# Four operand sums of w made in two halves each, and the row sums of |w| held back: a change to a matmul, tanh and multiply kernel

## The chip, the cores and the metric

The kernel runs on one core of a Trainium2 chip. The metric is the device time of one execution in microseconds (us), lower is better. The unchanged kernel has a median of 300.54 us over 6 runs (300.2 to 300.82).

## What is computed

```python
batch, m, k, n = 16, 512, 1024, 768
# x: (16, 512, 1024), w1 and w2: (1024, 768), all float32
y1 = np.matmul(x, w1)
y2 = np.matmul(x, w2)
return (np.tanh(y1) * y2).astype(np.float32)
```

With batch and m flattened, x has 8192 rows, which are 64 tiles of 128 rows. The inner dimension 1024 is 8 slices of 128.

## The kernel before

**Operands.** x and w are brought to f16. `wh` holds both weights, w1 in columns 0 to 767 and w2 in columns 768 to 1535, slice by slice. Slice k of w1 is loaded by the step `La{k}` and cast by `ca{k}`; `Lb{k}` and `cb{k}` do the same for w2 (L332 to L347). The loads are issued in the order x0 a0 x1 a1 x2 a2 x3 a3 a4 to a7 b0 to b7 (L538), so all of w1 comes ahead of w2. A cast may run on DVE or on ACT.

**Head.** The first six row tiles are multiplied plainly: `m{mt}{t}F{k}` is a matmul of 512 columns, `m{mt}{t}G{k}` one of the other 256, t = 0 for w1 and 1 for w2 (L447 to L449). x tiles 0 to 3 arrive as f32, are turned by TensorE (`PT{mt}{h}`, half h, L351) and moved from PSUM to SBUF as f16 by `e{mt}{h}` (a copy, L342 on ACT, L344 on DVE; `e10` is the first half of x tile 1). Tiles 4 and 5 are turned by `PT4`, `PT5` (L361). Then tanh of the first product (`thF`, `thG`, L455) and the multiplication with the second (`muF`, `muG`, L459) follow.

**Triples.** Row tiles 6 to 62 go in 19 groups of three (triples). Each triple is computed by a bilinear scheme with 15 products instead of the 18 that the plain way needs (`C_OPS`). A product is 4 matmuls of 128x512 (L477). Its operands are blocks of x and of w, or signed sums of blocks. Sums of x blocks (`S`, L434) are made anew for each triple. The eleven sums of w blocks (`B`, L424, listed in `B_SUMS`) are made once, 128x2048 f16 each, on DVE. Between the products, ACT makes copies of PSUM banks (`copy`, `seed`, L483) and tanh (L495), and DVE makes additions (L492) and the last multiplication (L500). The last row tile is plain again.

A w block is half of the slices by 512 columns. Blocks 1 and 8 are columns 0 to 511 of w1, 2 and 16 the same of w2, and 4 and 32 take the last 256 columns of w1 beside the last 256 of w2. So the first 256 columns of the sums 5, 36, 37 and 45 depend on w1 alone. In their other 256 columns, a block 4 or 32 takes part, and with it w2.

**Range check.** For every x tile and every slice of w, ACT sums absolute values (`D{mt}` and `awa{k}`, `awb{k}`, L390), an activation with an accumulator that writes a scratch tile `junk`. All these sums are looked at once, at the end; a general path would follow if they were out of range.

**Order.** A planner (`Planner.run`) lays out all steps before anything is issued. Each step has engines with a cost, a due time, steps that it needs, and steps that it only has to stand behind (`behind`). The planner fills each engine's queue in order of due times; the order of TensorE's products is fixed by hand (`PE_ORDER`). Each engine then runs its queue strictly in order. The eight PSUM banks are handed out by the planner: a bank is reused when its last reader is planned to be through. DMA loads of x (POOL queue), DMA transposes and stores (SP queue) have their own places in the plan.

Of the kernel before, what the change touches and what calls it, by code (L numbers as in the profile page):

```python
# [77 lines left out]
class Planner:  # L78
# [13 lines left out]
    def op(self, name, engines, due, needs, fn, *args, behind=(), issued=(), chains=(), xfer=0.0, latency=None, seeds=False):  # L92


        assert name not in self.ops, name
        self.ops[name] = dict(engines=engines, due=due, needs=[n for n in needs if n], behind=[n for n in behind if n], issued=[n for n in issued if n], fn=fn, args=args,
                              chains=chains, xfer=xfer, latency=latency, seeds=seeds)
        for c in chains:
            self.chains.setdefault(c, {"left": 0, "bank": None, "end": 0.0, "by": ""})["left"] += 1
# [134 lines left out]
def kernel(  # L234
# [19 lines left out]
    B, M, K = x.shape  # L254
    _, N = w1.shape
    KO = K // P
    KH = KO // 2
# [6 lines left out]
    LOW, HIGH = 512.0, 1024.0  # L264
    XT_BUFS, S_BUFS, O_BUFS, C_BUFS, WF_BUFS = 4, 2, 3, 2, 12
    WARM = 21
    AFTER = (0, 0, 0)
    SOON = {"S": 3.0, "D": 3.0}
    GATE = 2
# [31 lines left out]
    wsum = {v: once.tile([P, KH, F], f16, name=f"b{v}") for v, *_ in B_SUMS}  # L301
# [6 lines left out]
    pin = tc.keep_in_program_order  # L308
    engine = {"dve": nc.vector, "act": nc.scalar, "pool": nc.gpsimd, "sp": nc.sync}
    plan = Planner(8)  # L310
    op = plan.op
# [87 lines left out]
    def split(a):  # L399
        return a.rearrange("p k (t g) -> p k t g", t=2)  # L400

    def w_block(v):

        if v in wsum:
            return split(wsum[v])
        bit = v.bit_length() - 1
        rows = wh[:, bit // 3 * KH:(bit // 3 + 1) * KH, :]
        if bit % 3 == 2:
            return rows.rearrange("p k (t n) -> p k t n", t=2)[:, :, :, F:]
        return split(rows[:, :, bit % 3 * N:bit % 3 * N + F])  # L410
# [9 lines left out]

    OP = {"add": ALU.add, "sub": ALU.subtract}

    def w_sum(e, v, a, b, how):
        pin(engine[e].tensor_tensor(w_block(v), w_block(a), w_block(b), OP[how]))  # L424

    def x_operand(i, v):
        if v & (v - 1):
# [113 lines left out]
    for n, what in enumerate(loads):  # L541
# [5 lines left out]
        else:  # L547
            t = "ab".index(what[0])
# [3 lines left out]
    for a, t, k in slices:  # L552
        op(f"c{a}{k}", {"dve": 0.5, "act": 0.74}, 6 + 1.3 * k + 9.5 * t,
           [f"L{a}{k}"], cast_w, t, k)
        op(f"aw{a}{k}", {"act": 0.92}, 80 + 10 * (t * KO + k), [f"c{a}{k}"], abs_w, t, k)
    for mt in range(4):
        for h in range(2):
            due = 5 + 2.3 * mt + 0.1 * h
# [27 lines left out]
    def reuse_out(mt):  # L586
        return [f"st{mt - 3 * O_BUFS}"] if HEAD + 3 * O_BUFS <= mt else []
# [20 lines left out]
    for mt in list(range(4, HEAD)) + list(range(MT - TAIL, MT)):  # L608
# [6 lines left out]
        for n, (t, which) in enumerate(parts):  # L615
            last = plain(mt, t, which, (which, mt, t), lambda k: base + 1.7 * n + 0.2 * k,
                         behind=[plan.strict[FILL[n]]] if tail else ())
# [23 lines left out]
    for v, a, b, how in B_SUMS:  # L641
        needs = []
        for u in (a, b):
            if u in wsum:
                needs.append(f"B{u}")
            else:
                bit = u.bit_length() - 1
                needs += [f"c{s}{k}" for s in ("a", "b", "ab")[bit % 3] for k in range(bit // 3 * KH, (bit // 3 + 1) * KH)]
        op(f"B{v}", {"dve": 1.13}, None, needs, w_sum, v, a, b, how)

    def x_needs(i, v):
        if v & (v - 1):
# [12 lines left out]
    for i in range(TRIPLES):  # L665
        for v, a, b, how in A_SUMS:
            op(f"S{v}.{i}", {"pool": 1.12} if v in ON_POOL and i >= POOL_FROM else {"dve": 0.34}, None, x_needs(i, a) + x_needs(i, b), x_sum, i, v, a, b, how,
               behind=[f"{r}.{i - S_BUFS}" for r in a_readers[v]] if i >= S_BUFS else [])
# [3 lines left out]
        for o in C_OPS:  # L672
            name, kind, needs = o[:3]
            needs = [f"{n}.{i}" for n in needs]
# [22 lines left out]
            if kind in ("t", "th"):  # L697
                lo, n = (0, F) if kind == "t" else (F, G)
                op(f"{name}.{i}", {"act": 0.5 if n == F else 0.29}, due, needs, c_tanh, i, r, o[4], lo, n, o[5],
                   behind=reuse_out(mt), chains=chains)  # L700
# [11 lines left out]
    for mt in range(MT - TAIL - 3):  # L712
        op(f"st{mt}", {"sp": 0.05}, 52 + 4.33 * mt if mt >= HEAD else 250 + 5 * mt, outs[mt], store, mt,
           issued=[f"T{MT - 1}"] if mt < HEAD else [f"p{AFTER[(mt - HEAD) % 3]}.{(mt - HEAD) // 3 + 1}"], xfer=1.1)
    for mt in range(4, MT):
# [8 lines left out]
        else:  # L724
            op(f"T{mt}", {"sp": 1.35}, None, [f"L{mt}"], transpose, mt,
               issued=[f"T{mt - 1}"] if mt > BY_PE else [],
               behind=xt_readers[mt - 3 * XT_BUFS] if mt >= 3 * XT_BUFS else [], xfer=1.45, latency=2.2)
# [11 lines left out]
    pin(nc.vector.memset(ones, 2.0 ** -12))  # L739
    for n in range(WARM):  # L740
        pin(nc.tensor.matmul(banks[n % 8][:, n // 8 % 2 * 2 * P:][:, :2 * P], ones.bitcast(bf16)[:, :P], ones.bitcast(bf16), start=True, stop=True))  # L741
# [106 lines left out]
```

## Time and profile before

| what | value |
|---|---|
| median of 6 runs | 300.54 us |
| time of the profiled execution | 300.36 us |
| its span, first to last instruction | 298.5 us |
| mean granted TensorE clock | 0.997 |
| TensorE matmul (PE) busy | 292.6 us, 98% |
| TensorE weight load (PEld) busy | 139.8 us, 47% |
| VectorE (DVE) busy | 240.4 us, 81% |
| ScalarE (ACT) busy | 219.7 us, 74% |
| GpSimd (POOL) busy | 32.7 us, 11% |
| sums of w, L424 | 11 of 128x2048, 1215 to 1227 ns each, 24.5 to 51.8 us into the span |
| sums of abs(w), L390 | 16, median 844 ns each and a readout of 194 ns, 7.6 to 78.8 us into the span |

PE is TensorE's matmul row and PEld its weight loads, SPq, ACTq and POOLq are queues that issue DMAs. Times in the views are counted from the start of the span. A line such as L477 is the place in the kernel that issued an instruction.

### The profile page before, as it was taken

What the parts mean: (1) busy time and instruction counts of PE and PEld (TensorE: products, weight loads), DVE (VectorE), ACT (ScalarE), POOL (GpSimd) and SP (SyncE); (2) the same over time, 40 slices, a digit from 0 to 9 for tenths busy, and PEclk for the clock granted to TensorE, in tenths of its full rate; (3) what the DMA queues carried; (4) which work ended last, traced back from release to release, by engine and by line L of the source; (5) the groups of instructions that cost most, each with busy time, mean ns of one, the idle gap of its engine ahead of it and who ended that gap; (6) DMA issues with size and microseconds to landing.
All of it is one profiled execution on the core that took longest, in us unless ns stands there. A gap on an engine that the chain in (4) does not pass through costs nothing.

```text
span 298.5 us, 4459 instructions
## 1 busy us (share of the span) xinstructions
PE 292.6 (98%) x1418; PEld 139.8 (47%) x1418; DVE 240.4 (81%) x497; ACT 219.7 (74%) x438; POOL 32.7 (11%) x67
## 2 busy tenths in 40 slices
PE   8999999999999999999999999999999999999994
PEld 6656544444444444444444444444444444444442
DVE  1308999988988887888978979797898989888854
ACT  2879989999886868767787767777766777773641
POOL 0021211211002011110101111011011101000000
PEclk9999999999999999999999999999999999999998
DMA  7999999999999999999999999999999999996053
GB/s 282 409 399 210 161 175 147 185 136 263 190 191 124 294 238 236 247 299 128 246 86 210 250 246 248 202 236 140 195 232 252 124 284 233 167 374 267 19 231 124
DMA packets 82584, 64.79 MB, mean 217 GB/s; under 512 B 63616, under 2 KB 64128, under 8 KB 82560
## 3 DMA queue, kind: packets, MB, share of 16 engines
q1 hardware_dynamic: 73344, 47.20, 67.3%
q0 software_dynamic: 8640, 15.73, 37.9%
q10 hardware_dynamic: 576, 1.57, 1.3%
q8 instruction: 11, 0.18, 0.3%
q14 instruction: 13, 0.11, 0.2%
HBM read 39.85 MB, written 25.17 MB: 218 GB/s over the span
## 4 chain that ended last, share of the span: by engine, by line
PE 97%; ACT 1%; DVE 0%; issue 0%
PE bank L477 82%; PE bank L449 12%; PE bank L741 2%; ACT xT L342 1%; PE bank L351 1%; PE bank L361 0%; ACT junk L390 0%; DVE o L459 0%; DVE ones L739 0%; PE bank L515 0%
## 5 line engine op out<-in xcount | busy, mean ns | idle before, releaser
L477 PE MATMUL bank<-b,s 128*128 128x512 f16 x608 | 140.8, 379 | 0.0
L477 PEld LDWEIGHTS <-s 128*128 128x128 f16 x760 | 74.3, 98 | 89.6
L492 DVE TENSOR_TENSOR bank<-bank,s 128x512 f32<-128x512 f32 x95 | 66.2, 697 | 29.1 <-ACT s L483 22.2
L483 ACT ACTIVATE s<-bank 128x512 f32<-128x512 f32 x95 | 55.3, 597 | 42.2 <-PE bank L477 39.3
L390 ACT ACTIVATE junk<-xh 128x1024 f16<-128x1024 f16 x60 | 63.3, 1055 | 0.2
L500 DVE TENSOR_TENSOR o<-o,bank 128x256 f32<-128x256 f32 (+1 forms) x114 | 60.7, 548 | 2.2 <-ACT o L495 1.7
L477 PEld LDWEIGHTS <-xT 128*128 128x128 f16 x380 | 37.2, 98 | 44.6 <-issue 0.2
L477 PE MATMUL bank<-b,xT 128*128 128x512 f16 x228 | 55.4, 379 | 0.0
L384 POOL DMA_DIRECT2D xh<-in_x_dram x60 | 31.9, 533 | 198.8 <-ACT junk L390 107.7
L495 ACT ACTIVATE o<-bank 128x256 f32<-128x256 f32 x76 | 33.2, 438 | 10.0 <-DVE bank L492 6.5
L449 PE MATMUL bank<-wh,xT 128*128 128x512 f16 (+1 forms) x208 | 38.7, 338 | 0.9 <-ACT xT L342 0.7
L477 PE MATMUL bank<-wh,s 128*128 128x512 f16 x152 | 39.0, 379 | 0.0
L477 PE MATMUL bank<-wh,xT 128*128 128x512 f16 x152 | 39.0, 379 | 0.0
L434 DVE TENSOR_TENSOR s<-s,xT 128x512 f16<-128x512 f16 x76 | 31.8, 419 | 0.0
L449 PEld LDWEIGHTS <-xT 128*128 128x128 f16 x208 | 20.0, 98 | 17.6 <-ACT xT L342 1.6
L483 ACT ACTIVATE bank<-bank 128x512 f32<-128x512 f32 x38 | 20.4, 579 | 8.8 <-PE bank L477 7.2
L495 ACT ACTIVATE o<-s 128x512 f32<-128x512 f32 x38 | 23.9, 628 | 2.2 <-DVE s L492 2.0
L344 DVE CAST wh<-w_f 128x768 f16<-128x768 f32 x8 | 4.5, 564 | 18.5 <-DMA w_f<-in_w_dram 18.5
L434 DVE TENSOR_TENSOR s<-xT,s 128x512 f16<-128x512 f16 x38 | 16.0, 420 | 0.0
L434 DVE TENSOR_TENSOR s<-xT,xT 128x512 f16<-128x512 f16 x38 | 16.0, 420 | 0.0
L492 DVE TENSOR_TENSOR bank<-s,bank 128x512 f32<-128x512 f32 x19 | 13.1, 691 | 2.6 <-ACT o L495 2.5
L390 ACT ACTIVATE junk<-wh 128x768 f16<-128x768 f16 x16 | 13.6, 848 | 0.2
(39 smaller groups left out, 123.6 us busy)
## 6 DMA issues: line engine op xcount, KB each, us to landing
out_dram<-o SPq DMA_DIRECT2D x60, 384.0 KB, 5.8
xh<-in_x_dram POOLq DMA_DIRECT2D x60, 256.0 KB, 6.7
w_f<-in_w_dram SPq DMA_DIRECT2D x12, 384.0 KB, 8.1
x_f<-in_x_dram SPq DMA_DIRECT2D x4, 512.0 KB, 7.0
w_f<-in_w_dram ACTq DMA_DIRECT2D x4, 384.0 KB, 7.6
out_dram<-o SPq DMA_DIRECT2D x4, 256.0 KB, 2.3
xT<-xh SPq DMA_TRANSPOSE x58, 7.1
out_dram<-o SPq DMA_DIRECT2D x4, 128.0 KB, 2.0
```

Of the source, the lines that this page charges most:

```text
L342: pin(nc.scalar.copy(dst, src))
L344: pin(engine[e].tensor_copy(dst, src))
L384: pin(nc.gpsimd.dma_start(xhs[mt], xf[mt]))
L390: pin(nc.scalar.activation(junk[:, :src.shape[-1]], src, ACT.Abs, scale=scale, accum_out=sums[:, column:column + 1]))
L434: pin(engine[e].tensor_tensor(ss[i, v], x_operand(i, a), x_operand(i, b), OP[how]))
L449: pin(nc.tensor.matmul(b, xts[mt][:, k, :], rhs, start=first, stop=k == KO - 1, skip_group_check=True))
L477: pin(nc.tensor.matmul(place(i, dst), x_operand(i, a)[:, k, :], w_rhs(b, k), start=begins and k == 0, stop=k == KH - 1, skip_group_check=T ...
L483: pin(nc.scalar.activation(d, place(i, src), ACT.Copy, scale=float(sign)))
L492: pin(nc.vector.tensor_tensor(d, a, b, ALU.add if signs == (1, 1) else ALU.subtract))
L495: pin(nc.scalar.activation(out_tile(HEAD + 3 * i + r)[:, lo:lo + n], place(i, src)[:, :n], ACT.Tanh, scale=float(sign)))
L500: pin(nc.vector.tensor_tensor(o, o, place(i, src)[:, at:at + n], ALU.mult))
L741: pin(nc.tensor.matmul(banks[n % 8][:, n // 8 % 2 * 2 * P:][:, :2 * P], ones.bitcast(bf16)[:, :P], ones.bitcast(bf16), start=True, stop=True))
```

## The change

Two things are changed. The sums 5, 36, 37 and 45 become two steps each: `B{v}a` makes columns 0 to 255 and needs only casts of w1 (`ca`) and first halves of other sums; `B{v}` makes columns 256 to 511 and needs what the whole sum needed, and `B{v}a`. Each has a planner cost of 0.6 in place of 1.13. The other seven sums stay whole. And every sum of |w| (`aw`) has to stand behind the product p0 of the second triple (`p0.1`).

```diff
+    BY_HALF = (5, 36, 37, 45)
...
-    def w_sum(e, v, a, b, how):
-        pin(engine[e].tensor_tensor(w_block(v), w_block(a), w_block(b), OP[how]))
+    def w_sum(e, v, a, b, how, t=slice(0, 2)):
+        pin(engine[e].tensor_tensor(w_block(v)[:, :, t], w_block(a)[:, :, t], w_block(b)[:, :, t], OP[how]))
...
-        op(f"aw{a}{k}", {"act": 0.92}, 80 + 10 * (t * KO + k), [f"c{a}{k}"], abs_w, t, k)
+        op(f"aw{a}{k}", {"act": 0.92}, 80 + 10 * (t * KO + k), [f"c{a}{k}"], abs_w, t, k, behind=["p0.1"])
...
-        op(f"B{v}", {"dve": 1.13}, None, needs, w_sum, v, a, b, how)
+        if v not in BY_HALF:
+            op(f"B{v}", {"dve": 1.13}, None, needs, w_sum, v, a, b, how)
+            continue
+        first = []
+        for u in (a, b):
+            if u in wsum:
+                first.append(f"B{u}a")
+            else:
+                row = (u.bit_length() - 1) // 3 * KH
+                first += [f"ca{k}" for k in range(row, row + KH)]
+        op(f"B{v}a", {"dve": 0.6}, None, first, w_sum, v, a, b, how, slice(0, 1))
+        op(f"B{v}", {"dve": 0.6}, None, needs + [f"B{v}a"], w_sum, v, a, b, how, slice(1, 2))
```

Since the planner lays everything out anew, other steps move too. In the order lists of the two built kernels, per engine:

- TensorE has the same instructions in the same order up to the turning of x tile 5; behind it six of the plain matmuls of tiles 4 and 5 change places and some products use other PSUM banks.
- DVE runs, behind the casts of w1 slices 0 to 3, the first half of sum 5, then `e31` (which ACT had), then the first halves of 36, 37 and 45, and then the casts of w2. The cast of w1 slice 4, which DVE had, goes to ACT. The second half of 5 stands between two casts of w2, and whole and half sums of w fill the stretch up to the multiplications of the head.
- ACT no longer has sums of |w| between `e01` and `e10`, `e11` and `e20`, `e21` and `e30`. It has all 16 of them behind `p0.1`, four in each of the next four rounds of 15 products.
- POOL and SP have the same lists in the same order.

## The prediction

> **What bounds the kernel now.** I read the chain that ended last, first as shares and then in order of time.
>
> ```profile
> 7.74 0.84 ACT junk L390 x2
> 8.57 0.48 ACT xT L342
> 9.05 0.05 issue
> 9.10 1.15 PE bank L449 x6
> ...
> 14.04 14.03 PE bank L449 x86
> ...
> 46.68 227.07 PE bank L477 x1052
> ```
>
> Columns are start, length, what. From 13.16 to 294.53 us the chain is TensorE alone. The long piece holds 1052 matmuls of 512 columns in 227.07 us, 0.2158 us from one start to the next. The product lines around it keep the same pace: 4 matmuls in 0.86. In the windows view PE is busy for the whole of every stretch from 14 to 290 us at a granted clock of 1.00. So there is nothing to win behind the head unless an instruction of TensorE goes, and none does. The time can only fall by TensorE's idle time in the head.
>
> The Trainium skill, page Perfetto Trace Analysis, section Identifying the Most-Contended Engine, warns that a busy matmul row does not tell how near TensorE is to its limit; weight-load share does. Weight loads are 47% here, which by that rule leaves room. The row decides otherwise: 0.2158 is what the page VectorE: DVE Perf Modes (section The TRN2 errata) gives for 512 columns, 518 cycles at 2.4 GHz. By the one there might be gaps for the change to fill, by the other there are none.
>
> The waits of PE, beside the warm-up's, are one line, and the timeline shows the weight loads' part of a third gap:
>
> ```profile
> PE bank L449 <- ACT xT L342: 0.7, 2, 0.5
> ```
>
> ```profile
> 22.21 0.10 PEld L449 LDWEIGHTS <-xT 128*128 128x128 f16 x1
> 22.49 0.10 PEld L449 LDWEIGHTS <-xT 128*128 128x128 f16 x1 [0.18 <-issue]
> ```
>
> Two waits come before 12 us (0.47 at 9.10 and 0.24 at 11.37, in the timeline). The third is small: 0.28 between two loads where 0.22 is the pace, so 0.06 us lost. What released it? The instruction at 22.49 is `m21F0`, which takes the PSUM bank that the first tanh (`thF0`) reads. The ACT rows of that stretch:
>
> ```profile
> 20.28 1.66 ACT L342 CAST wh<-w_f 128x768 f16<-128x768 f32 x2 [1.47 <-DMA w_f<-in_w_dram]
> 21.85 1.08 ACT L455 ACTIVATE o<-bank 128x512 f32<-128x512 f32 x2
> ```
>
> The first tanh runs 21.85 to 22.44, and 0.05 later TensorE goes on. It stands behind the casts of w2 slices 2 and 3, and those wait for DMA: ACT idles 1.47 us for the first, and the second starts at 21.11, 0.02 behind its landing at 21.09. All of w arrives at 400 GB/s (14 to 22 us). So there is a gate at 22.49 which a DMA landing sets, and TensorE is only 0.06 us early at it.
>
> **Part 1: the halved sums.** Nobody waits for the sums of w: the view of their line has an empty list under "who waited for it". In before, sum 37 ends at 31.5 us and its product p9.0 starts at 44.2. Making them earlier gains 0.
>
> The same page of the skill (Perfetto Trace Analysis, Optimizing Scalar/DVE Operations) says that breaking up instructions can finish work sooner where an engine that is not saturated causes bubbles on others. DVE does idle 8.45 us ahead of the cast at 22.09, but no bubble of another engine is caused by these sums; by the rule there could be a gain, by the view there is none.
>
> Cost: a whole sum (2048 elements) takes 1.22 us, 1.135 from start to start; an x sum (512) takes 0.42 and 0.335. The line through both is 0.068 + 0.52 ns per element, so a half (1024) is 0.60 and two halves 1.20. Four sums cost 4 x 0.07 = 0.27 us more of DVE. The sliced 4x256 form is not in the trace; its bounds are the two rows, 0.335 and 1.135. Even at 1.135 the first half of 5 and `e31` end by 14.9, and the other three first halves, which wait for the cast of w1 slice 7 (ends near 16.95), end by 20.4, inside DVE's idle 13.64 to 22.09. This idle hides them: 0. Behind 22 us DVE has the same sums in another order, 2.4 us less of them, and the multiplications of the head start up to 1.5 us later (the second one near 33.6 instead of 32.0); their banks are asked for at 34 to 38 us. I take 0; without that cover a sum's half, 0.6, would be the price.
>
> **Part 2: the sums of |w| leave the head.** Three of them stood in front of x copies on ACT. `awa0` (7.63 to 8.48) delays `e10`: the first four of the eight transposes at 7.59 end at 8.19 (fourth start 7.92, each 0.27), and ACT follows TensorE by 0.04, so `e10` could start at 8.23 instead of 8.47. Then TensorE's 9.10 becomes 8.86: 0.24 us earlier. `awa1` costs nothing (ACT idles 0.35 behind it), nor does `awa2` (1.01). The wait at 11.37 stays as long as it is, 0.24 earlier: the copy follows its transposes at once. The x tiles and casts needed on the way are there (x2 lands 9.57, needed 9.85; x3 11.83, needed 12.77; w1 slice 3 is cast at 12.90, needed 13.64).
>
> But at the gate TensorE would now come at 22.19, and the first tanh still ends at 22.44, because the casts ahead of it still wait for the same landings. So the gap there grows from 0.06 to 0.30 and takes back the whole 0.24. This is the step on which the forecast turns. What is late next is the landing of w2 slice 3. Behind the gate the next three banks are freed 0.16, 0.10 and 0.05 us before they are asked for, as in before.
>
> **Part 3: what moves.** `e31` on DVE costs 0.6 to 0.69 (rows: 0.59 on ACT, 0.69 for 1024 columns on DVE); the transposes end at 13.80, so it ends by 14.5, and its first reader comes at 16.56. The cast of w1 slice 4 on ACT (0.83) ends at 14.7 instead of 13.64; first reader 15.91. From slice 7 on, ACT waits for landings as before. POOL and SP have the same lists; x loads wait for a transposition's landing plus 0.56 us (32.23, issue 32.79), not for a row sum, so none of it moves. The swapped matmuls of tiles 4 and 5 have the same count and size: 0.
>
> **Part 4: the sums of |w| in the triples.** ACT gets four more in each of four rounds (15 products, 12.95 us), from about 66 to 114 us. The windows view:
>
> ```profile
> 51.00:64.00 13.00, 13.00 (x61) 5.86 (x60) 12.02 (x25) 12.48 (x29) 2.11 (x4) 1.00 1.12 171
> ...
> 103.00:116.00 13.00, 13.00 (x62) 5.88 (x60) 11.25 (x25) 9.79 (x20) 1.58 (x3) 1.00 1.15 241
> ```
>
> The fourth figure is ACT: 9.79 of 13 with no sum of |w|, 12.48 with three, and PE (first) loses nothing in either. With four: a sum takes 0.97 from start to start ahead of another row sum (46.66 to 47.62) and 0.84 ahead of a copy (47.62 to 48.47); two of each are 3.62. The rest, packed: 7 copies at 0.48, 3 tanh at 0.50, 3 short ones at 0.27, 3 row sums of x at 1.05, and 0.15 where a sum of |w| follows one (54.02 to 55.23 is 1.21): 8.97. Together 12.59 of 12.95. It fits, with 0.36 per round and about 0.8 us that a copy such as `seed56` ends ahead of its product. Upper bound: 4 x 0.97 on the 9.79 as measured is 13.67, 0.72 too much in each round, 2.9 us, less the 0.8: +2.1 us. Lower bound: 0. I take 0, the packed sum being made of start-to-start rows.
>
> In the stretch they leave (38 to 51 us) a product waits 0.02 us for a copy at 51.71; that goes: -0.02.
>
> **Sum.** -0.24 at `e10`, +0.24 at the gate, 0 for parts 1 and 3, 0 for part 4, -0.02: the profiled 300.36 (span 298.5 and 1.86 around it) becomes 300.34. The median shown is 0.18 above that execution, so 300.5 on its footing.
>
> **Rivals.** (a) Forecast, 300.5: chance 0.80. (b) The gate does not hold: w2 slice 3 lands 0.2 us or more earlier against TensorE in most executions, so the 0.24 is kept, 300.3. For it: the margin is 0.06 us. Against it: x and w come in one stream, which sets both sides of the gate. Chance 0.09. (c) Slower: ACT overloaded in the four rounds. It decides when a sum of |w| costs more than (12.95 - 8.97) / 4 = 0.995 us on the average, against 0.905 from the rows. TensorE then waits for `seed56` in front of p14, once per round. At 1.05 each that is 4 x 0.22 = 0.9 less the 0.8 in hand, +0.1 to +0.3; at the bound +2.1, 302.6. For it: the load is 97%, with engines strictly in order. Against it: 12.48 of 13 was borne without a loss. Chance 0.10, of which over +0.6 us 0.07. (d) The change doesn't do what it says: the first halves wait until w2 is there, since DVE runs in order. That would put 2.4 us back into 25 to 45 us, where nobody waited: 300.5 too, inside (a). The last 0.01 is left for what I do not see.
>
> About 0.2%, 0.6 us, is what a measurement of this kernel can tell from no change. Faster by more would take over twice the idle time within reach: 0.02. Slower by more: 0.08, from (c). Within: 0.90. The range goes from 300.1 (b with the spread of 0.2 below the median) to 301.0 (a mild c).
>
> **What would show it.** Right: `e10` starts near 8.23 and TensorE goes on near 8.86; the gap at 22.49 is 0.3 us with the tanh at 21.85 still behind casts that wait for DMA; first halves of the sums between 13 and 20 us; PE without a gap from 22.5 to the end. Wrong: no gap at the gate (b), or PE waits for L483 between 70 and 115 us (c).

## The result and the profile after

The changed kernel takes 301.05 us (median of 21 runs, 300.26 to 303.77), the kernel before, beside it, 300.47 (42 runs). The ratio is 1.002, 95% interval 1.001 to 1.0029: slower by about 0.6 us. The profiled execution takes 301.26 us with a span of 299.5 and a granted clock of 1.00, against 300.36 and 298.5.

The chain that ended last, in order of time (start, length, what), is no longer TensorE alone behind 13 us:

```profile
16.16 10.78 DMA w_f<-in_w_dram
26.94 0.02 issue
26.96 0.84 ACT wh L343
27.80 0.02 issue
27.82 2.96 DVE b L425 x3
30.79 0.60 DVE xT L345
31.39 2.22 DVE b L425 x3
33.61 0.56 issue
34.17 0.68 DVE o L460
34.86 0.61 DVE xT L345
35.47 0.04 issue
35.51 3.62 PE bank L450 x16
...
47.54 227.06 PE bank L478 x1052
```

(Lines stand one later than before from L266 to L648: L343 and L345 are the moves and casts on ACT and DVE, L425 the sums of w, L460 the multiplication, L450 the plain matmul, L478 the product.) The long piece is the same 1052 matmuls in 227.06 us, so nothing is lost in the triples. It starts at 47.54 instead of 46.68. Everything is decided before that, and the chain says by what: the last slice of w2 lands at 26.94, is cast on ACT, and from there DVE works through sums of w, the move `T4` of x tile 4, more sums, the first multiplication `muF0` and the move `T5` of x tile 5, without a break. Two matmuls wait for it. PE's list of waits names one of them, in its third line (engine, line, releaser: us in total, times, longest):

```profile
PE bank L450 <- ACT xT L343: 0.7, 3, 0.2
PE bank L450 <- ACT o L456: 0.4, 1, 0.4
PE bank L450 <- DVE xT L345: 0.2, 1, 0.2
```

Before, only the first of these lines was there beside the warm-up. The second is the gate at 22.5 us, the third is new. This list leaves out what it puts down to "issue". The weight loads show both waits; the idle time between two of them is 0.12 us at full pace (0.2158 less 0.10):

```profile
34.91 0.10 PEld L450 LDWEIGHTS <-xT 128*128 128x128 f16 x1 [0.42 <-issue]
35.51 0.96 PEld L450 LDWEIGHTS <-xT 128*128 128x128 f16 x5 [0.51 <-issue]
```

From the starts of single matmuls, what is beyond the pace of 0.2158 us is a gap (`M` stands for 512 columns made of the last 256 of w1 and of w2):

| where TensorE loses time | before: start, gap | after: start, gap |
|---|---|---|
| goes on behind `e10` | 9.10 | 8.80 |
| goes on behind `e20` | 11.37 | 11.06 |
| `m21F0`, the gate | 22.49, 0.06 | 22.66, 0.54 |
| `m40M0`, bank that `muF0` empties | none | 34.91, 0.31 |
| `m41F0`, bank that `T5` empties | none | 35.51, 0.39 |
| a product behind a copy on ACT | 51.71, 0.02 | none |

-0.31 + 0.48 + 0.69 - 0.02 = +0.84 us. The last matmul ends at 295.38 instead of 294.53, +0.85, and the profiled times differ by 0.90. The account closes for these two executions: the gain of the head is more than given back at the gate, and 0.69 is lost in two new waits. Head and gate are not the slowdown, though. The kernel before, executed once more (e12 below), lost 0.71 at its gate, and two variants of the changed kernel (e5, e6) lose 0.53 and 0.59 there and still take the time of before. What sets the changed kernel apart is the 0.69.

**Why DVE is late.** Its timeline in the changed kernel (start, length, operation, number of instructions, in brackets the idle time before and what ended it):

```profile
25.22 1.22 DVE L425 TENSOR_TENSOR b<-wh 128x2048 f16<-128x2048 f16 x1
27.82 1.83 DVE L425 TENSOR_TENSOR b<-wh 128x2048 f16<-128x2048 f16 x2 [1.38 <-ACT wh L343]
29.57 1.22 DVE L425 TENSOR_TENSOR b<-wh,b 128x2048 f16<-128x2048 f16 x1
30.70 0.69 DVE L345 COPY xT<-bank 128x1024 f16<-128x1024 f16 x1
31.30 0.68 DVE L425 TENSOR_TENSOR b<-wh,b 128x1024 f16<-128x1024 f16 x1
31.90 1.22 DVE L425 TENSOR_TENSOR b<-b,b 128x2048 f16<-128x2048 f16 x1
33.04 1.22 DVE L425 TENSOR_TENSOR b<-wh 128x2048 f16<-128x2048 f16 x1
34.17 0.68 DVE L460 TENSOR_TENSOR o<-o,bank 128x512 f32<-128x512 f32 x1
34.77 0.69 DVE L345 COPY xT<-bank 128x1024 f16<-128x1024 f16 x1
```

At 27.82 DVE has idled 1.38 us for the cast of the last w2 slice, because sum 24, the first here that needs it, is next in its queue. Behind it stand sums 36, 26, `T4`, 37, 29, 18, `muF0` and `T5`, and all of them come late. In the kernel before, the order was 36, `T4`, 24, 37, `muF0`, `muF1`, `T5`, and there was idle time in it, ahead of both moves (the last of the first two sums here is 36):

```profile
25.65 2.35 DVE L424 TENSOR_TENSOR b<-wh 128x2048 f16<-128x2048 f16 x2
28.55 0.69 DVE L344 COPY xT<-bank 128x1024 f16<-128x1024 f16 x1 [0.55 <-PE bank L361]
29.16 1.22 DVE L424 TENSOR_TENSOR b<-wh 128x2048 f16<-128x2048 f16 x1
30.30 1.22 DVE L424 TENSOR_TENSOR b<-wh,b 128x2048 f16<-128x2048 f16 x1
31.43 1.28 DVE L459 TENSOR_TENSOR o<-o,bank 128x512 f32<-128x512 f32 x2
32.90 0.69 DVE L344 COPY xT<-bank 128x1024 f16<-128x1024 f16 x1 [0.19 <-PE bank L361]
```

TensorE's order at tile 4 moved too. `m40M0` was the second matmul of the tile and is the ninth now. The tenth, `m41F0`, now has the bank that `T5` empties and asks for it near 34.8; before, it had the bank that `muF1` empties and came at 36.16, and the bank of `T5` was first used at 36.37, by `m50F0`.

**Why the slice is late.** The issue of the first x loads of the triples hangs on a step `gate` of the kernel: POOL copies one column of the raw w2 slice number `GATE` = 2, and the x loads stand behind this copy in POOL's queue. POOL's rows, first of the kernel before, then of the changed one:

```profile
20.31 0.18 POOL L521 COPY held<-w_f 128x1 f32<-128x1 f32 x1 [19.00 <-DMA w_f<-in_w_dram]
20.43 2.87 POOL L384 DMA_DIRECT2D xh<-in_x_dram  x5
```

```profile
19.07 0.18 POOL L522 COPY held<-w_f 128x1 f32<-128x1 f32 x1 [17.76 <-DMA w_f<-in_w_dram]
19.19 2.79 POOL L385 DMA_DIRECT2D xh<-in_x_dram  x5
```

The gate opens 1.24 us earlier, and five x loads of 256 KB come in beside the last w2 slices. The eight slices land at 16.97, 17.96, 20.26, 21.09, 22.07, 23.07, 24.02 and 25.05 us before, and at 17.08, 18.05, 19.02, 21.26, 22.23, 23.25, 24.72 and 26.94 after. In each list one of the slices 1 to 5 comes 2.2 or 2.3 us behind its predecessor instead of 1.0: slice 2 before, slice 3 after. When it is slice 3, the gate on slice 2 opens early; the last two slices are then 1.47 and 2.22 behind their predecessors, and the last one lands 1.9 us later.

The rest is as forecast in kind. The gate of the first tanh shows on ACT:

```profile
21.29 0.83 ACT L343 CAST wh<-w_f 128x768 f16<-128x768 f32 x1 [1.41 <-DMA w_f<-in_w_dram]
22.02 2.32 ACT L456 ACTIVATE o<-bank 128x512 f32<-128x512 f32 x5
```

The cast of slice 3 waits 1.41 us for its DMA, and the tanh stands behind it. And in the triples that took over the sums of |w| (windows view: window, its length, busy time and instructions of PE, PEld, DVE, ACT and POOL, then clock, DMA share, GB/s), PE is busy throughout with ACT at 96 and 97%:

```profile
66.00:79.00 13.00, 13.00 (x62) 5.91 (x61) 11.16 (x25) 12.49 (x28) 1.20 (x3) 1.00 1.03 205
79.00:92.00 13.00, 13.00 (x62) 5.85 (x60) 11.08 (x25) 12.63 (x29) 1.63 (x4) 1.00 1.09 217
```

### The profile page after: what moved, and what is told of

Same layout as the page of the kernel before. It is cut to its first block, busy times and chain, and to the rows that moved or that the text cites. A ratio compares the mean times of both kernels' runs of the same rounds, so it can differ in the third digit from the quotient of the medians.

```text
span 299.5 us, 4447 instructions
## 1 busy us (share of the span) xinstructions
PE 292.8 (98%) x1418; PEld 139.1 (46%) x1418; DVE 240.7 (80%) x501; ACT 219.4 (73%) x438; POOL 32.6 (11%) x67
## 4 chain that ended last, share of the span: by engine, by line
PE 87%; DMA 8%; DVE 3%; issue 0%; ACT 0%; ACTq 0%; SPq 0%
PE bank L478 82%; DMA w_f<-in_w_dram 8%; PE bank L450 5%; DVE b L425 2%; DVE xT L345 0%; DVE o L460 0%; ACT wh L343 0%; ACTq L339 0%; SPq L339 0%; PE bank L516 0%
## 5 line engine op out<-in xcount | busy, mean ns | idle before, releaser
L478 PE MATMUL bank<-b,s 128*128 128x512 f16 x608 | 140.9, 380 | 0.0
L478 PEld LDWEIGHTS <-s 128*128 128x128 f16 x760 | 74.2, 98 | 89.6
L478 PEld LDWEIGHTS <-xT 128*128 128x128 f16 x380 | 37.1, 98 | 44.7
L478 PE MATMUL bank<-b,xT 128*128 128x512 f16 x228 | 55.4, 380 | 0.0
L450 PE MATMUL bank<-wh,xT 128*128 128x512 f16 (+1 forms) x208 | 39.2, 339 | 1.5 <-ACT xT L343 0.7
L478 PE MATMUL bank<-wh,xT 128*128 128x512 f16 x152 | 39.0, 380 | 0.0
L478 PE MATMUL bank<-wh,s 128*128 128x512 f16 x152 | 39.0, 380 | 0.0
L450 PEld LDWEIGHTS <-xT 128*128 128x128 f16 x208 | 20.0, 98 | 18.7 <-issue 1.6
L345 DVE CAST wh<-w_f 128x768 f16<-128x768 f32 x7 | 3.9, 559 | 13.2 <-DMA w_f<-in_w_dram 13.2
```

The costliest lines, as they stand in the source:

```text
L345: pin(engine[e].tensor_copy(dst, src))
L450: pin(nc.tensor.matmul(b, xts[mt][:, k, :], rhs, start=first, stop=k == KO - 1, skip_group_check=True))
L478: pin(nc.tensor.matmul(place(i, dst), x_operand(i, a)[:, k, :], w_rhs(b, k), start=begins and k == 0, stop=k == KH - 1, skip_group_check=T ...
```

## The experiments

T1, from the traces: the loss comes when two things meet, a late landing of the last w2 slice and a DVE queue in which a sum that waits for this slice stands ahead of `muF0` and `T5`. The expectations set rivals against it: ACT loaded with the sums of |w| in the triples (the prediction's rival (c)), the chance of one execution's landings whatever the kernel, the halves by their number and form, and the shared DMA by itself. Each kernel was timed beside the kernel before on the same chip. "Last slice" is the landing of w2 slice 7, "gap" the TensorE time lost at the place named, both from the profiled execution; losses at the gate near 22.6 are not in the table.

| run | median, before | ratio (95%) | last slice | gap at `m40M0` + `m41F0` |
|---|---|---|---|---|
| e1_halves_only | 300.90, 300.56 | 1.0016 (1.0007 to 1.0024) | 25.30 | 0 |
| e2_aw_only | 300.56, 300.56 | 1.0005 (0.9995 to 1.0016) | 25.34 | 0 |
| e3_after_gate1 | 301.70, 300.56 | 1.0035 (1.0022 to 1.0048) | 27.19 | 0.69 + 0.39 |
| e4_before_gate1 | 301.84, 300.56 | 1.004 (1.0026 to 1.0054) | 27.40 | 0 (0.06 at 33.03, 0.82 at 50.11) |
| e5_late_sums | 300.58, 300.62 | 0.9996 (0.9987 to 1.0005) | 26.87 | 0 |
| e6_after_gate3 | 300.58, 300.62 | 0.9997 (0.9988 to 1.0006) | 25.09 | 0 |
| e7_order_only | 300.62, 300.62 | 1.0004 (0.9995 to 1.0013) | 25.24 | 0 (0.12 at 33.15) |
| e8_after_again | 301.16, 300.62 | 1.0016 (1.0007 to 1.0025) | 26.80 | 0.30 + 0.39 |
| e9_late_gate1 | 300.56, 300.57 | 0.9996 (0.9987 to 1.0005) | 27.69 | 0 |
| e10_aw_gate1 | 301.57, 300.57 | 1.0027 (1.0015 to 1.0038) | 28.86 | 1.12 at 34.49 |
| e11_best | 300.06, 300.57 | 0.9983 (0.9974 to 0.9992) | 26.51 | 0 |
| e12_before_again | 300.76, one run | – | 25.38 | 0 |

### One part of the change alone

e1: the changed kernel without the rule for the sums of |w|.

```diff
-        op(f"aw{a}{k}", ..., abs_w, t, k, behind=["p0.1"])
+        op(f"aw{a}{k}", ..., abs_w, t, k)
```

> The changed kernel with its sums of |w| back where they were in before, so only the halved sums of w remain. Theory 1 (DVE's queue: the new order puts whole sums of w, one of which waits for the last slice of w2, in front of the first multiplication of the head and of the move of x tile 5, and TensorE waits for both): TensorE waits in front of the second and third block of tile 4's matmuls, near 34.9 and 35.5 us, by about 0.3 and 0.4 us whenever the last slice of w2 lands near 27 us, and not when it lands near 25. Median 0.4 to 0.9 us above before. Theory 2 (rival: the later sums of |w| overload ACT in the triples): same time as before, within 0.1 us, no such waits. Theory 3 (the extra waiting is the chance of one execution's landings, no matter what kernel): same as before within 0.1 us in the median.

e2: the kernel before with that rule and whole sums.

```diff
-        op(f"aw{a}{k}", ..., abs_w, t, k)
+        op(f"aw{a}{k}", ..., abs_w, t, k, behind=["p0.1"])
```

> Before with the sums of |w| held behind p0 of the second triple, no sum halved. Theory 1: no wait at 33 to 36 us even if w2's last slice lands near 27 us, since DVE's order there is that of before; TensorE goes on near 8.85 instead of 9.10 and loses the 0.24 again at the gate near 22.5 to 22.7, where the first tanh frees a bank; time as before, -0.2 to +0.1 us. Theory 2: 0.4 to 0.9 us slower, with waits for ACT's copies (L483) between 66 and 115 us. Theory 3: as before.

e2 is not slower. Its trace has TensorE going on at 8.88 instead of 9.10 and 0.49 us lost at the gate: this is what the prediction's part 2 says, but e12 below shows differences of this size between two executions of the kernel before, so one trace is no proof. The moved sums of |w| cost nothing that the time shows, and no matmul waits between 60 us and the end (one product waits 0.14 us at 58.08). So an ACT overload is refuted. e1 is slower by 0.16% and holds the cost, though its profiled execution (300.79) had an early last slice and no gap at tile 4. Its eleven executions fall into 300.62 to 300.91 (seven) and 301.27 to 301.68 (four). That would be the 0.69 us of T1 in four of them, but no trace of one of those four was taken.

### The landing moved in the changed kernel

```diff
-    GATE = 2
+    GATE = 1
```

> The changed kernel with the gate of the x loads set on slice 1 of w2 instead of slice 2, so that the loads of x tiles 4 to 8 start near 18.2 us in every execution and share the DMA engines with the last slices of w2. Theory 1: the last slice lands at 27 us or later always; the waits of TensorE at tile 4 are there in every execution, 0.7 us or more together, and the median is 0.2 to 1.5 us above that of the changed kernel (301.05). Theories 2 and 3: no more than 0.2 us above the changed kernel.

```diff
-    GATE = 2
+    GATE = 3
```

> The changed kernel with the gate of the x loads on slice 3 of w2, so that they start near 21.2 us at the earliest, in every execution. Theory 1: the last slice of w2 lands near 25.2 us always, the waits at 34.9 and 35.5 us are gone, the median is 300.3 to 300.6 us, and no execution stands out by 0.5 us. Rival (halves cost by themselves): 0.3 us or more above before, as the changed kernel is.

In e3 the x loads start at 18.30, the last slice lands at 27.19, and the first gap grows from 0.31 to 0.69. From the time at which TensorE passes the gate to the landing it is 4.28 us in the changed kernel and 4.66 in e3, 0.38 more; the wait grew by 0.39. So TensorE waits one for one for the landing, as far as two traces tell. In e6 the x loads start at 21.38, the slice lands at 25.09, and with the same instructions in the same order the gaps at tile 4 and the 0.5 us are gone. `T5` ends there at 33.71 and its bank is asked for at 34.77: 1.06 us of slack, which a landing 1.9 us later uses up. T1 has both. The halves are all in e6, and it takes the time of before, so they cost nothing by their number and form.

### The landing moved in the kernel before

```diff
-    GATE = 2
+    GATE = 1
```

> Before with the same early gate on slice 1 of w2. Theory 1: the last slice of w2 lands at 27 us or later here too, but DVE has fewer sums in front of its multiplications, so TensorE loses 0 to 0.3 us at tile 4; the later row sums of ACT may cost up to 0.5 us near 50 us; the median is less above before (0 to 0.8 us) than the changed kernel with this gate is. Theory 3 (late landing costs any kernel alike): as much above before as the changed kernel with this gate, 0.8 us or more, with the waits at the same matmuls.

The expectation was missed: the kernel before loses as much as the changed one does in e3, but not at tile 4. PE's list of waits names another place:

```profile
PE bank L477 <- ACT s L483: 0.7, 1, 0.7
```

It is a product at 50.11 that waits for a copy on ACT, which stood behind sums of |w| (in ACT's timeline the copy runs from 49.48 to 50.06, with two sums of |w| right ahead of it, at 47.67 and 48.64). Would the kernel with the sums of |w| moved away then be safe? e10 adds that rule:

```diff
-    GATE = 2
+    GATE = 1
...
-        op(f"aw{a}{k}", ..., abs_w, t, k)
+        op(f"aw{a}{k}", ..., abs_w, t, k, behind=["p0.1"])
```

> Before with the sums of |w| held back, no sum halved, and the early gate on slice 1 of w2. Theory 1: the last slice lands past 27 us; the row sums no longer stand in front of the ACT copy near 50 us, where before with this gate lost 0.82 us; DVE has few sums ahead of the head's multiplications, so 0 to 0.2 us at 33 us; median 300.5 to 300.9. Rival (sharing the DMA engines costs time by itself): 301.5 or more.

Missed again: 301.57 is a time that the rival named. The wait at 50 us is gone, as it should be, but the last slice lands at 28.86 here, the gate costs 0.84, and a new wait appears at 34.49:

```profile
PE bank L449 <- DVE o L459: 1.0, 1, 1.0
```

`L459` is `muF0`. In the order of before, too, sums that need the last slice (36, 24, 37) stand ahead of it. With a landing at 27.40 (e4) `muF0` makes TensorE wait 0.06, with 28.86 it is 1.12. So the difference between the orders is one of slack: by these traces the changed order pays from a landing near 26.2 on (26.94 less the 0.69 paid; 27.19 less 1.08 in e3), the order of before from about 27.3 (27.7 in e10, where TensorE passes its gate 0.4 us later than in e4). I had taken its slack for larger. e4 and e10 speak for the second half of T1 (who stands behind the landing) and against my reading that the kernel before was immune. That the rival's time doesn't come from sharing the DMA engines is shown by e9 below, with the same early gate on the same chip.

### The order on DVE changed, the landing left

e5 is the changed kernel, with six whole sums put behind `T5`, among them the four (24, 26, 29, 18) that stood ahead of `muF0` beside sum 6:

```diff
-            op(f"B{v}", {"dve": 1.13}, None, needs, ...)
+            op(f"B{v}", {"dve": 1.13}, None, needs, ...,
+               behind=["T5"] if v in (18, 24, 26, 27, 29, 48) else [])
```

> The changed kernel, but six whole sums of w (18, 24, 26, 27, 29, 48) have to stand behind the move of x tile 5 on DVE, so the first multiplications of the head and that move come earlier in DVE's queue. Theory 1 (DVE's queue): no wait of TensorE at 33 to 36 us however late the last slice of w2 lands; the median falls from that of the changed kernel to that of before, 300.3 to 300.6 us. Rival (the halves cost by themselves, by their number and form): stays 0.3 us or more above before.

The last slice is as late as in the changed kernel (26.87), and DVE idles for it just as long, but what stands behind is less (DVE's timeline):

```profile
27.76 0.69 DVE L425 TENSOR_TENSOR b<-wh 128x1024 f16<-128x1024 f16 x1 [1.38 <-ACT wh L343]
28.48 0.69 DVE L425 TENSOR_TENSOR b<-wh,b 128x1024 f16<-128x1024 f16 x1
29.21 0.69 DVE L425 TENSOR_TENSOR b<-b,wh 128x1024 f16<-128x1024 f16 x1
29.82 0.68 DVE L345 COPY xT<-bank 128x1024 f16<-128x1024 f16 x1
31.48 1.28 DVE L460 TENSOR_TENSOR o<-o,bank 128x512 f32<-128x512 f32 x2 [0.98 <-PE bank L450]
33.01 0.69 DVE L345 COPY xT<-bank 128x1024 f16<-128x1024 f16 x1 [0.25 <-PE bank L362]
```

`muF0` starts at 31.48 instead of 34.17 and waits for TensorE, not TensorE for it. No gap at tile 4, time 0.9996 of before. The planner's answer to this edit goes further than DVE: TensorE's matmuls of tile 4 have the order and banks of before again, `m40M0` at 33.03 and `m41F0` at 36.26 on the bank that `muF1` empties. So e5 tests DVE's order and TensorE's together; which share of the 0.69 is due to `m41F0` taking the bank of `T5` was not tried apart. e8 ran the changed kernel once more, unedited, beside it:

> The changed kernel once more, beside the others on one chip. Theory 1: median 0.3 to 0.9 us above before with executions in two groups, those near 300.6 and those from 301.0 up; its profile has either the last slice of w2 near 25 us and no wait at 34.9 and 35.5, or near 27 us and both.

301.16 against 300.58 on one chip: both waits are there again, 0.30 and 0.39. (The two groups of executions that were expected are not clear: they go from 300.55 to 301.65 without a break of over 0.32.) With a landing as late in e5 as in e8, this tells T1 from the shared DMA by itself. e9 drives it further, e5 with `GATE = 1`:

```diff
-    GATE = 2
+    GATE = 1
```

> The kernel with halved sums, later sums of |w| and six whole sums behind the move of x tile 5, now with the early gate (slice 1 of w2), so that the last slice of w2 lands past 27 us in every execution. Theory 1 (the loss is DVE's queue at tile 4, and in before with this gate it is the row sums in front of an ACT copy near 50 us): both weak places are gone, no wait at 33 to 36 nor at 50 us, median 300.4 to 300.8, 1 us below the changed kernel and before with the same gate (301.70 and 301.84). Rival (sharing the DMA engines costs time by itself): 301.5 or more.

With a last slice at 27.69 there is still no gap at tile 4 or near 50 us, and the time is that of before, 1.0 us below e10 with the same gate. Neither the late landing nor the shared DMA costs anything where no order makes TensorE wait for it.

e7 is the kernel before with sums 18, 24, 26 and 29 due earlier, so that they stand ahead of `muF0`:

```diff
-        op(f"B{v}", {"dve": 1.13}, None, needs, ...)
+        op(f"B{v}", {"dve": 1.13}, 25 if v in (18, 24, 26, 29) else None, needs, ...)
```

> Before, no sum halved, sums of |w| where they were, but the whole sums 18, 24, 26 and 29 given an early due time, so that DVE has B5 B24 B18 B29 B26, the move of x tile 4 and B36 ahead of the first multiplication. Theory 1: slower though nothing is halved: TensorE waits near 33 to 35 us in front of tile 4's second block, about 0 us if the last slice of w2 lands near 25 and 1.5 to 1.9 us if it lands near 27; median 0.1 to 1.9 us above before. Rival (halves cost by themselves): as before, within 0.1 us.

Inconclusive: the profiled execution has an early last slice (25.24), 0.12 us lost at 33.15, and the median is that of before. The order alone is cheap as long as the slice is early, which T1 says too, but the other half was not seen.

### A version that beats both

The forecast's first half said that the head gains about 0.3 us and loses it at the gate, since the first tanh stands on ACT behind casts that wait for DMA. If so, these casts on DVE should keep the gain. e11 is e5 with the casts of w2 slices 2 and 3 on DVE only; the planner also puts a few of TensorE's matmuls between 21 and 24 us in another order (`m21F0` at 21.45, `m11F2` at 23.84):

```diff
-        op(f"c{a}{k}", {"dve": 0.5, "act": 0.74}, 6 + 1.3 * k + 9.5 * t,
+        op(f"c{a}{k}", {"dve": 0.5} if t and k in (2, 3) else {"dve": 0.5, "act": 0.74}, 6 + 1.3 * k + 9.5 * t,
```

> The kernel with halved sums, later sums of |w| and six whole sums behind the move of x tile 5, with the casts of w2 slices 2 and 3 on DVE alone. The tanh of the head no longer stands behind them on ACT. Theory of the gate: the 0.5 us that TensorE loses near 22.6 us goes, nothing else moves, and the time is 0.3 to 0.5 us below before: 300.1 to 300.3. Rival (the gate is TensorE's own pace, tanh follows the matmuls at once): the gap stays 0.3 us or more and the time is that of before.

ACT's timeline in e11:

```profile
20.14 3.17 ACT L456 ACTIVATE o<-bank 128x512 f32<-128x512 f32 x8 [1.25 <-PE bank L450]
```

The first tanh starts at 20.14 and waits for TensorE alone. TensorE goes on at 8.78 and 11.04, and behind that there is no gap to the end. The edit and the new order of the matmuls work together here and were not tried apart. 300.06 us, ratio 0.9983 (0.9974 to 0.9992). Of the 0.5 us, 0.33 is the earlier 11.04 and 0.08 the two small gaps that the first trace of before had (0.06 and 0.02); the last 0.1 I can't place.

e12 is one more execution of the kernel before, unedited:

> Before once more, one look. The question is when slices 2, 3 and 7 of w2 land. If the slot that lands late is a matter of chance, slice 2 or 3 may be the late one here. Theory 1: whichever it is, TensorE does not wait at 33 to 36 us; if slice 3 is the late one and the x loads start near 19.2, the last slice lands near 26.9 and TensorE loses up to 0.5 us near 50 us, where row sums stand in front of an ACT copy.

300.76: slice 2 late again (20.36), and yet TensorE goes on at 8.71, earlier than in the changed kernel. The copies of x tile 0 start at 6.27 here and at 6.62 in the first trace of this kernel, so the sum of |w| ahead of `e10` is over earlier too: it ends at 8.09, the transposes that `e10` needs end at 7.92, and `e10` starts at 8.07. It is delayed by about 0.1 us here, not 0.24. At the gate 0.71 us is lost. So both the cost of that sum and the gap at the gate differ from one execution of the same kernel to the next.

## Why the prediction was wrong, step by step

**Right: what bounds the kernel.** Nothing is lost or won behind 47.54 us; the 1052 products take 227.06 us against 227.07.

**Right, but less firm than it was told: the head.** `e10` starts at 8.16 (forecast 8.23), TensorE goes on at 8.80 (8.86), 0.30 earlier (0.24). The other runs give the spread. From the landing of x tile 1 until TensorE goes on it takes 1.37 to 1.42 us in eight of the nine traces with the sums of |w| held back, and 1.54 in e2; with these sums in the head it is 1.49 (e12), 1.53 (e1), 1.68 (e7), 1.78 (before) and 1.93 (e4). The gain is there, 0.3 on the average, with e2 and e12 as the pair that shows none; one trace gave one size of it.

**Right in kind, too small: the gate.** Forecast 0.30 us with the tanh ending at 22.44; measured 0.54, the tanh ending near 22.6, since slice 3 landed at 21.26 instead of 21.09. Of the 0.24 more, 0.17 is this later tanh. This term was +0.24 and measured +0.48, but the trace that it was counted from had a lucky gate: the kernel before loses 0.06 there in one execution and 0.71 in another (e12), since the landings differ. That head and gate together come to about 0, as forecast, is borne out by the times of e2, e5 and e6 (1.0005, 0.9996, 0.9997). In e11 the tanh is no longer behind a cast, and the gap is gone.

**Right: the price of the halves.** Start to start a half is 0.60 where independent work follows and 0.72 to 0.73 where the next instruction needs its result (16.98, 17.71, 18.43), within the bounds. The first halves ran at 13.04 to 19.1, in DVE's idle time. The Trainium skill, page Perfetto Trace Analysis, section Optimizing Scalar/DVE Operations, says that breaking up instructions of Scalar or Vector may finish work sooner where these engines are not saturated but cause bubbles on others. No engine waited for these sums before, so the condition was not met. The trace has the first halves done by 19.1 us; the other instructions were then reordered around them, and that had the price.

**Wrong: "I take 0" behind 22 us in part 1.** This is the step that failed, and with it 300.5 us became 301.05. I had seen that the multiplications of the head start later, the second one near 33.6 instead of 32.0 (with an early slice, in e6, it does start at 33.63), and set against it that "their banks are asked for at 34 to 38 us". Two things were missed. First, the queue was shifted with the landings of one execution held fixed. The sums that moved forward wait for the last slice, and its landing moves with the gate of the x loads, 25.05 in one trace and 26.94 in the other. Second, I looked at the multiplications and not at the move `T5`, which stands behind `muF0` in the new order, and whose bank now goes to `m41F0`, which asks for it only about 1 us after `T5` ends even with an early slice (e6). In place of this 0 the profile has 0.31 for `muF0` and 0.39 for `T5`. The price that I gave for lost cover, 0.6, is near the 0.69 paid by chance: it was the length of a half sum, not a wait for a late slice. A landing of the last slice past 26 us should have been a rival with a price in the range.

**Right: parts 3 and 4.** `e31` on DVE at 13.85 and the cast of w1 slice 4 on ACT at 13.82 delayed nothing. Of the ACT overload, rival (c), nothing is seen: no gap behind 36 us in the changed kernel, and e2 at 1.0005. Nor did rival (b) come: the gate held.

**Open.** Which slice comes 2.2 us behind its predecessor decides when the x loads start. Of the seven traces of kernels with both parts of the change, it was slice 3 in six (the changed kernel, e3, e5, e6, e8, e11) and slice 2 in e9. Of the seven others it was slice 2 in six (before, e1, e2, e7, e10, e12) and slice 3 in e4. One thing goes with the halves in the traces: the instruction fetch named below starts at 18.26 to 18.52 us in the eight traces with halved sums and at 17.60 to 18.10 in the six without. Whether the change itself shifts the late slice was not settled: executions without a profile show no landings, and the medians mix them. That the new order turns a late last slice into 0.69 us is shown (e6 and e3, the same order with other landings; e5 against e8, the same landing with another order). That the change makes a late one more frequent is only argued.

## What to carry to other kernels

An engine that runs in order passes every wait on to all that stands behind it, so when a change moves an instruction forward, ask first what it waits for and only then how long it takes; work that waits for a DMA belongs behind the work that frees PSUM banks (e5 against e8, 0.6 us). When a planner hands out banks anew, ask again which instruction frees each bank and when it is next used. Give each landing that the new order hangs on a range, not the time of one trace, and compare its late end with the slack of the bank that is asked for first. A gain ahead of a gate is kept only by the edit that also moves the gate (e11).

## What the runs showed of the hardware beside this

- In all fourteen traces slice 2 or slice 3 of w2 (384 KB) lands 2.2 to 2.6 us behind its predecessor, where 1.0 is the pace (the last slices do so too where the x loads have come in), and the trace has an instruction fetch of 16 KB that takes 1.1 us and starts 2.2 to 3.0 us ahead of that landing (at 18.10 us before and 18.51 after; the late slices land at 20.26 and 21.26). That the one causes the other is argued from their times; it was not tried.
- The earlier the five x loads of 256 KB start, the later the last slice of w2 lands, though it was issued near 16.1 us and ahead of them. With one and the same order of instructions: loads from 21.38 us on, landing at 25.09 (e6); from 19.19, 26.94 (the changed kernel); from 18.30, 27.19 (e3).
